# Sums of weight quarters in the first MLP matrix: accumulating transfers in a chain in place of VectorE's subtractions

## The chip, the cores and the metric

One core of a Trainium2 chip runs the whole program. The metric is the device time of one execution in microseconds (us); lower is better. The engines of the core are TensorE (PE; its weight loads are PEld), VectorE (DVE), ScalarE (ACT), GpSimd (POOL) and SyncE (SP). Each works through its own instructions in order and waits on semaphores for the others. SP and POOL also issue transfers between device memory and the on-chip memory, each into a queue of its own.

## What is computed

One layer of a decoder trunk on 512 tokens of width 2048: token mixing by a convolution and an attention branch, then a squared-ReLU MLP, with RMSNorm ahead of each and at the end. The change lies in the MLP's first product, `h @ w_ff1`, a matrix of 512 x 2048 times one of 2048 x 8192.

```python
def reference(x, g_mix, w_in, b_f, b_gate, conv_w, w_conv_out, w_attn_out,
              w_mix_out, g_mlp, w_ff1, w_ff2, g_final):
    ...
        h = rmsnorm(x, g_mlp[l])
        u = jnp.square(jax.nn.relu(jnp.einsum('bsd,df->bsf', h, w_ff1[l])))
        x = x + jnp.einsum('bsf,fd->bsd', u, w_ff2[l])
    return rmsnorm(x, g_final)
```

All inputs and the output are float32.

## The kernel before, in words

Every large product is done in 2 x 2 quarters with seven quarter products in place of eight (the scheme of Strassen and Winograd). The seven are named after the factor on the side of the activations: A11, A12, S1, S2, S3, S4, A22. A11, A12 and A22 are quarters of the activations, S1 to S4 sums and differences of them, made once and kept on chip (`Blocks.sums`, L796). The weights' quarters and their sums and differences are made anew for each block of columns.

Such a block is a `Group` (L173). For `w_ff1` there are 16 groups, g = 0 to 15, of 512 columns each. A group loads four weight quarters of 128 x 2048 floats (1 MB) by `load` (L182, SP's queue) into tiles x00, x10, x01 and x11, which take turns in four slots: `free` lists the free ones, `done` gives one back. A tile in a slot is loaded again only once everything that reads the old one has ended.

For each quarter product `run` (L194) splits its weight operand into two parts whose sum is the operand (`split`, L99): ScalarE copies it to `th` in the shorter format fp32r (L100), and VectorE takes the difference `tl` (L101). `th` and `tl` have two buffers each. Then TensorE does 48 matmuls of 128 x 128 by 256 columns (`mm_cols`, L144 to L148): 32 with `th`, 16 with `tl`. In the groups from 1 on one spare matmul stands ahead of S2 (L631).

The weight operands that are no plain quarters are made in place by VectorE with `sub` (L104), four a group, each 128 x 2048: in `tail` (L252) for groups 1 to 15, in `tail2` (L283) for group 0. `head` (L227) does A11 and A12. The order of the products is A11, A12, S4, S2, S3, S1, A22 in groups 1 to 15 and A11, A12, S1, S3, S2, S4, A22 in group 0.

The products accumulate in four PSUM banks a, b, c, d. `snap` (L205) copies a bank to a tile `o`, `plus` (L107) adds another bank to it, and `put` hands a finished quarter of the result to `put_u` (L872). That applies ReLU (L904), squares (L876), makes the sums that the second MLP matrix needs in a tile `r`, splits it into `rh` (L892) and the rest in `r` (L893), and stores both to device memory through POOL's queue (L895, L896; 896 KB each, two pairs a group). There is one tile `r` and one `rh`. `load_sums` (L938) loads them again, as `us`, through POOL's queue for the second matrix.

The instructions are given out in program order with priorities by a scheduler, so that an engine's order is fixed when the program is built.

## Time and profile before

| what | value |
|---|---|
| median of 2 runs | 2461.64 us (2461.31 to 2461.97) |
| the profiled execution, its own time | 2459.11 us |
| its span, first to last instruction | 2457.4 us |
| granted TensorE clock over the span | 0.998 |
| HBM read, written | 368.16 MB, 92.27 MB |
| the stage of the change (groups 0 to 15) | about 1230 to 1835 us |

The span is the time of the profiled execution from the first instruction to the last; 1.7 us of its own time lie around it. Busy times of engines overlap. Where one engine is busy without a gap, the others' idle time costs nothing, and a shorter instruction of theirs gains nothing unless that engine waits for it. A row of a view that groups instructions gives line, engine, operation, output and inputs, shapes, the number, then busy time in us and the mean duration of one in ns, then the idle time just before them.

### The profile page before, as it was taken

To read this page: it belongs to the slowest core of one execution; us is meant where nothing else is said; L and a number is where in the kernel's file an instruction comes from. 1 tells how busy PE (TensorE), PEld (TensorE's weight loads), DVE (VectorE), ACT (ScalarE), POOL (GpSimd) and SP (SyncE) were. 2 spreads that over 40 slices of the span, in tenths; PEclk is the share of its full clock that TensorE was granted. 3 is DMA by queue.
4 is the path that set the end of the run, shared out by engine and by line. 5 is a ranking of instruction groups with operands and counts; after the bars stand their busy time and mean duration, and the time that the engine had idled before them with its cause. 6 is when DMAs were issued, how large, how long until landed. Compare 5 with 4: busy or idle time off the path is not lost.

```text
span 2457.4 us, 39283 instructions
## 1 busy us (share of the span) xinstructions
PE 2431.6 (99%) x16928; PEld 2247.3 (91%) x16928; DVE 1921.1 (78%) x1592; ACT 1149.1 (47%) x1147; POOL 180.0 (7%) x280
## 2 busy tenths in 40 slices
PE   8999999999999999999999999999999999999998
PEld 8999999999999988888899999999998888888886
DVE  7887777788777744425688898988988888889898
ACT  6443443334444532225556666666665333333334
POOL 0100000001000000000000000000011001100000
PEclk9999999999999999999999999999999999999999
DMA  7564544456534554335645646556488576655662
GB/s 249 182 191 143 165 128 138 155 168 210 163 118 149 176 180 142 128 137 190 204 144 202 237 178 228 198 201 235 172 298 299 169 253 223 239 187 184 246 224 102
DMA packets 272036, 463.00 MB, mean 188 GB/s; under 512 B 10269, under 2 KB 172181, under 8 KB 271733
## 3 DMA queue, kind: packets, MB, share of 16 engines
q1 hardware_dynamic: 235136, 303.13, 38.3%
q0 software_dynamic: 35856, 156.25, 16.9%
q8 instruction: 133, 2.18, 0.4%
q10 hardware_dynamic: 868, 1.10, 0.1%
q14 instruction: 43, 0.34, 0.0%
HBM read 368.16 MB, written 92.27 MB: 187 GB/s over the span
## 4 chain that ended last, share of the span: by engine, by line
PE 95%; DVE 3%; issue 1%; ACT 1%; DMA 1%; POOL 0%; SPq 0%; DVEq 0%; POOLq 0%; ACTq 0%
PE a L148 6%; PE a L144 6%; PE a L146 6%; PE a L162 5%; PE a L164 5%; PE a L161 5%; PE d L148 5%; PE d L144 5%; PE d L146 5%; PE c L146 4%; PE c L144 4%; PE c L148 3%; PE d L162 3%; PE d L164 3%; PE d L161 3%; PE b L144 2%
## 5 line engine op out<-in xcount | busy, mean ns | idle before, releaser
L100 ACT ACTIVATE th<-x 128x2048 fp32r<-128x2048 f32 (+1 forms) x252 | 483.2, 1918 | 506.3 <-DVE x L104 156.5
L101 DVE TENSOR_TENSOR tl<-x,th 128x2048 fp32r<-128x2048 f32 (+1 forms) x252 | 575.6, 2290 | 172.1 <-ACT th L100 157.9
L104 DVE TENSOR_TENSOR x<-x,x 128x2048 f32<-128x2048 f32 (+1 forms) x144 | 329.7, 2289 | 8.3 <-DMA x<-in_w_in_dram 6.2
L100 ACT ACTIVATE th<-y 128x2048 fp32r<-128x2048 f32 x81 | 155.6, 1922 | 227.7 <-PE a L162 138.7
L101 DVE TENSOR_TENSOR tl<-raw,th 128x2048 fp32r<-128x2048 f32 x40 | 91.7, 2293 | 150.7 <-ACT th L100 150.1
L161 PE MATMUL a<-th,us 128*128 128x512 f32 x512 | 199.2, 389 | 0.0
L162 PE MATMUL a<-th,us 128*128 128x512 f32 x512 | 199.2, 389 | 0.0
L101 DVE TENSOR_TENSOR tl<-y,th 128x2048 fp32r<-128x2048 f32 x81 | 185.1, 2288 | 16.8 <-ACT th L100 16.6
L144 PE MATMUL a<-ST,th 128*128 128x256 f32 x752 | 173.4, 277 | 0.8 <-ACT th L100 0.8
L146 PE MATMUL a<-ST,th 128*128 128x256 f32 x752 | 172.9, 276 | 0.0
L100 ACT ACTIVATE th<-raw 128x2048 fp32r<-128x2048 f32 x40 | 76.7, 1918 | 176.3 <-PE pt L345 71.5
L144 PEld LDWEIGHTS a<-ST,th 128*128 128x128 f32 x752 | 141.2, 188 | 1.1 <-ACT th L100 1.0
L146 PEld LDWEIGHTS a<-ST,th 128*128 128x128 f32 x752 | 141.2, 188 | 0.0
L164 PE MATMUL a<-tl,us 128*128 128x512 f32 x512 | 136.7, 389 | 0.0
L144 PE MATMUL c<-S,th 128*128 128x256 f32 x576 | 134.6, 278 | 0.0
L146 PE MATMUL c<-S,th 128*128 128x256 f32 x576 | 134.4, 278 | 0.0
L100 ACT ACTIVATE th<-t 128x2048 fp32r<-128x2048 f32 x31 | 59.5, 1919 | 125.3 <-DVE t L104 73.0
L144 PE MATMUL d<-ST,th 128*128 128x256 f32 x512 | 117.7, 276 | 0.0
L146 PE MATMUL d<-ST,th 128*128 128x256 f32 x512 | 117.6, 276 | 0.0
L162 PEld LDWEIGHTS a<-th,us 128*128 128x128 f32 x512 | 96.1, 188 | 20.0
L164 PEld LDWEIGHTS a<-tl,us 128*128 128x128 f32 x512 | 96.0, 188 | 20.0
L161 PEld LDWEIGHTS a<-th,us 128*128 128x128 f32 x512 | 96.1, 188 | 20.0
(298 smaller groups left out, 6384.0 us busy)
## 6 DMA issues: line engine op xcount, KB each, us to landing
x<-in_w_in_dram SPq DMA_DIRECT2D x86, 1024.0 KB, 5.7
x<-in_w_ff_dram SPq DMA_DIRECT2D x64, 1024.0 KB, 7.2
y<-in_w_ff_dram SPq DMA_DIRECT2D x64, 1024.0 KB, 7.7
us<-s_d POOLq DMA_DIRECT2D x48, 1024.0 KB, 9.0
s_d<-rh POOLq DMA_DIRECT2D x32, 896.0 KB, 5.6
s_d<-r POOLq DMA_DIRECT2D x32, 896.0 KB, 5.8
raw<-in_w_mix_out_dram SPq DMA_DIRECT2D x24, 1024.0 KB, 5.1
g_d<-o POOLq DMA_DIRECT2D x32, 256.0 KB, 2.7
```

Source lines behind the costliest of these rows:

```text
L100: nc.scalar.activation(out=hi, in_=src, func=AF.Copy)
L101: nc.vector.tensor_tensor(out=lo, in0=src, in1=hi.bitcast(F32), op=ALU.subtract)
L104: nc.vector.tensor_tensor(out=out, in0=a, in1=b, op=ALU.subtract)
L144: nc.tensor.matmul(o, hi[:, q, js], Sh, start=first and q == 0 and j == 0, stop=False, skip_group_check=True)
L146: nc.tensor.matmul(o, hi[:, q, js], Sl, start=False, stop=False, skip_group_check=True)
L148: nc.tensor.matmul(o, lo[:, q, js], Sh, start=False, stop=q == nq - 1, skip_group_check=True)
L161: nc.tensor.matmul(o, Sh, hi[:, q, :], start=begin and q == 0, stop=False, skip_group_check=True)
L162: nc.tensor.matmul(o, Sl, hi[:, q, :], start=False, stop=False, skip_group_check=True)
L164: nc.tensor.matmul(o, Sh, lo[:, q, :], start=False, stop=q == nq - 1, skip_group_check=True)
```

## The change

The weight sums of `w_ff1` are no longer made on VectorE. A new method `chained` does a whole group:

- x00 becomes a chain. It holds the plain quarter for A11. When its split has been read, a transfer from device memory adds quarter (0, 1) onto it, which gives the weight operand of S1; after that one's split a second transfer adds (1, 1), for S2; then a third adds (1, 0), for A22. A separate transfer adds (1, 1) onto x01, for S3. So each group has four loads as before and four accumulating transfers (`onto`) of 1 MB, issued on POOL's queue.
- All weight operands are now plain sums. The signs that they had go to the activations (in `Blocks.sums` one addition becomes a subtraction and one the reverse) and to the results (`minus`, and a negative scale in a snapshot).
- The order of the products is A11, A12, S1, S3, S2, S4, A22 in all 16 groups, so that each second product reads the chain.
- In groups 1 to 15 all four quarters are loaded ahead; in group 0 (`ahead=False`) two of them. The load of the first `us` in the last group moves from behind `head` to behind the `put` of the first result quarter, which is the same place between A12 and the third product.

```diff
+        def minus(self, s, ps, scale=1.0):
+
+            p = ps[0][:, :2 * self.w].rearrange("p (b c) -> p b c", b=2)
+            if scale == 1.0:
+                sub(s, s, p)
+            else:
+                nc.vector.scalar_tensor_tensor(out=s, in0=p, scalar=-scale, in1=s, op0=ALU.mult, op1=ALU.add)
+
+        def onto(self, t, i, j):
+
+            c = self.cs[j]
+            src = self.view[:, c:c + self.w].rearrange("(q two p) c -> two p q c", two=2, p=P)
+            nc.gpsimd.dma_start(out=t, in_=src[i], accum_op=ALU.add)
...
+        def chained(self, between=lambda: None, behind=lambda: None, ahead=True):
+            X = self.X = {}
+            for ij in ((0, 0), (1, 0), (0, 1), (1, 1))[:4 if ahead else 2]:
+                X[ij] = self.load(*ij)
+            if ahead:
+                self.onto(X[0, 1], 1, 1)
+            chain = X[0, 0]
+            a = self.acc("a")
+            self.run(a, "A11", chain, True)
+            self.onto(chain, 0, 1)
+            s1 = self.snap(a)
+            between()
+            b = self.acc("b")
+            self.run(b, "A12", X[1, 0], True)
+            self.done(1, 0)
+            self.plus(s1, b)
+            self.put(0, 0, s1)
+            behind()
+            if not ahead:
+                X[0, 1], X[1, 1] = self.load(0, 1), self.load(1, 1)
+                self.onto(X[0, 1], 1, 1)
+            c = self.acc("c")
+            self.run(c, "S1", chain, True)
+            self.onto(chain, 1, 1)
+            d = self.acc("d")
+            self.run(d, "S3", X[0, 1], True)
+            self.done(0, 1)
+            d1 = self.snap(d, -self.scale)
+            self.plus(d1, c, self.scale)
+            self.run(a, "S2", chain, False)
+            self.onto(chain, 1, 0)
+            s2 = self.snap(a)
+            while later:
+                later.pop(0)()
+            self.minus(d1, a, self.scale)
+            self.put(1, 1, d1)
+            self.run(c, "S4", X[1, 1], False)
+            self.done(1, 1)
+            s4 = self.snap(c, self.scale)
+            self.minus(s4, a, self.scale)
+            self.put(0, 1, s4)
+            self.run(d, "A22", chain, False)
+            self.done(0, 0)
+            self.plus(s2, d)
+            self.put(1, 0, s2)
...
             self.put("A22", c, a22)
-            add(a22, a21, a22)
+            sub(a22, a21, a22)
...
-            sub(a12, a12, a11)
+            add(a12, a12, a11)
...
-    g0.head(True, rest)
-    Q2.sums(3)
-    g0.tail2()
+    g0.chained(rest, lambda: Q2.sums(3), ahead=False)
...
-        group.head(True, order=((0, 0), (0, 1), (1, 0)))
-        if g == DFF // S - 1:
-            us0 = {}
-            load_sums(0, (0,), us0)
-        group.tail()
+        us0 = {}
+        group.chained(behind=(lambda: load_sums(0, (0,), us0)) if g == DFF // S - 1 else lambda: None)
```

Where this puts the instructions, at three places of one pair of groups, 7 and 8. A row gives the line (the changed kernel's lines stand some 60 later than those above, L236 is `onto`, L958 and L959 are the stores of `rh` and `r`), the operation, output and inputs with their buffer numbers, the output's shape, and what the instruction waits for.

POOL before, from the first store in group 7 on:

```order
L895 DMA s_d3_79<-rh_14628 128x1792 [waits DMASW0_49,Activation_49]
L896 DMA s_d3_79<-r_14620 128x1792 [waits DMASW1_49,DVE_49]
L895 DMA s_d3_79<-rh_14926 128x1792 [waits DMASW2_49,Activation_49]
L896 DMA s_d3_79<-r_14918 128x1792 [waits DMASW3_49,DVE_49]
L895 DMA s_d3_79<-rh_15054 128x1792 [waits DMASW4_49,Activation_49]
```

POOL now, from the first link of group 7 (x00_14694 is its chain, x00_15121 and x01_15125 belong to group 8) on:

```order
L236 DMA x00_14694<-in_w_ff1_dram 128x8x256 [waits DMAHW5_49,DMAHW2_49,DVE_49]
L958 DMA s_d3_79<-rh_14634 128x1792 [waits DMASW6_49,Activation_49]
L959 DMA s_d3_79<-r_14626 128x1792 [waits DMASW7_49,DVE_49]
L236 DMA x00_14694<-in_w_ff1_dram 128x8x256 [waits DMASW5_49]
L958 DMA s_d3_79<-rh_14988 128x1792 [waits DMASW1_49,Activation_49]
L959 DMA s_d3_79<-r_14980 128x1792 [waits DMASW2_49,DVE_49]
L236 DMA x00_14694<-in_w_ff1_dram 128x8x256 [waits DMASW3_49,DMASW0_49,DVE_49]
L236 DMA x01_15125<-in_w_ff1_dram 128x8x256 [waits DMAHW0_49,DMAHW3_49,DMASW4_49,DVE_49]
L236 DMA x00_15121<-in_w_ff1_dram 128x8x256 [waits DMAHW6_49,DMAHW1_49,DVE_49]
L958 DMA s_d3_79<-rh_15061 128x1792 [waits DMASW6_49,Activation_49]
L959 DMA s_d3_79<-r_15053 128x1792 [waits DMASW7_49,DVE_49]
L236 DMA x00_15121<-in_w_ff1_dram 128x8x256 [waits DMASW5_49,DVE_49]
```

Where only stores stood, two a pair, there are now a group's four accumulating transfers among them in one queue. In group 7 the second link stands behind both stores of the pair before it, and group 8's first two transfers stand behind the third link of group 7.

VectorE before, in group 7 from the split of S4's operand on (x11_14804 and x10_14692 are weight quarters, x00_14688 is S1's operand):

```order
L101 TENSOR_TENSOR tl_14808<-x11_14804,th_14807 128x2048 [waits PE_49,Activation_49]
L893 TENSOR_TENSOR r_14620<-r_14620,rh_14628 128x1792 [waits Activation_49]
L104 TENSOR_TENSOR x11_14804<-x11_14804,x00_14688 128x2048 [waits DVE_49]
L107 TENSOR_TENSOR o_14747<-b_14749,o_14747 128x512 [waits PE_49]
L104 TENSOR_TENSOR x10_14692<-x10_14692,x11_14804 128x2048 [waits DVE_49]
L101 TENSOR_TENSOR tl_14863<-x11_14804,th_14862 128x2048 [waits Activation_49]
L101 TENSOR_TENSOR tl_14935<-x01_14690,th_14934 128x2048 [waits PE_49,Activation_49]
L107 TENSOR_TENSOR r_14918<-o_14490,r_14918 128x256 [waits DMASW1_49,Activation_49]
L104 TENSOR_TENSOR r_14918<-r_14918,o_14490 128x256
L104 TENSOR_TENSOR r_14918<-r_14918 128x256 [waits DVE_49] x2
L101 TENSOR_TENSOR tl_14989<-x00_14688,th_14988 128x2048 [waits PE_49,Activation_49]
L893 TENSOR_TENSOR r_14918<-r_14918,rh_14926 128x1792 [waits Activation_49]
```

VectorE now, in group 7 from the split of S1's operand on:

```order
L101 TENSOR_TENSOR tl_14816<-x00_14694,th_14815 128x2048 [waits DMASW5_49,PE_49,Activation_49]
L956 TENSOR_TENSOR r_14626<-r_14626,rh_14634 128x1792 [waits Activation_49]
L107 TENSOR_TENSOR o_14757<-b_14759,o_14757 128x512 [waits PE_49,Activation_49]
L101 TENSOR_TENSOR tl_14870<-x01_14698,th_14869 128x2048 [waits DMASW4_49,Activation_49]
L104 TENSOR_TENSOR r_14980<-r_14980,o_14551 128x256 [waits DMASW7_49,DVE_49,Activation_49]
L107 TENSOR_TENSOR r_14980<-o_14551,r_14980 128x256 [waits Activation_49]
L104 TENSOR_TENSOR r_14980<-r_14980 128x256 [waits DVE_49] x2
L956 TENSOR_TENSOR r_14980<-r_14980,rh_14988 128x1792 [waits Activation_49]
L101 TENSOR_TENSOR tl_14925<-x00_14694,th_14924 128x2048 [waits DMASW0_49,PE_49,Activation_49]
L101 TENSOR_TENSOR tl_14998<-x11_14700,th_14997 128x2048 [waits DMAHW0_49,PE_49,Activation_49]
L107 TENSOR_TENSOR o_14921<-c_14814,o_14921 128x512 [waits Activation_49]
L104 TENSOR_TENSOR o_14921<-o_14921,a_14703 128x512 [waits DVE_49,Activation_49]
```

The two subtractions of weight tiles among these splits are gone. What stands behind `tl` of S1 (x00_14694) is the remainder of `r` for the store that POOL has ahead of the next link. A new `r` can be begun only once the last one's store has landed, and it stands ahead of `tl` of S2.

ScalarE before, at the end of group 8, from the operand of S1 to the square of the next result:

```order
L100 ACTIVATE th_15414<-x00_15114 128x2048 [waits DVE_49,PE_49]
L892 ACTIVATE rh_15352<-r_15344 128x1792 [waits DMASW4_49,DVE_49,Activation_49]
L205 ACTIVATE o_15342<-a_15120 128x512 [waits PE_49]
L100 ACTIVATE th_15485<-x10_15118 128x2048 [waits PE_49]
L205 ACTIVATE o_15412<-d_15359 128x512 [waits PE_49]
L100 ACTIVATE th_15547<-x00_15540 128x2048 [waits DMAHW5_49,DVE_49,PE_49]
L205 ACTIVATE o_15466<-a_15120 128x512 [waits PE_49]
L904 ACTIVATE o_15412<-o_15412,common_11671 128x512 [waits DVE_49]
L876 ACTIVATE r_15472<-o_15412 128x256 [waits DMASW7_49,Activation_49]
L876 ACTIVATE o_15412<-o_15412 128x256
```

ScalarE now, at the end of group 8, from the operand of S2 to A11 of group 9 (x00_15548):

```order
L100 ACTIVATE th_15351<-x00_15121 128x2048 [waits DMASW0_49,PE_49]
L955 ACTIVATE rh_15415<-r_15407 128x1792 [waits DMASW6_49,DVE_49]
L100 ACTIVATE th_15424<-x11_15127 128x2048 [waits DMAHW4_49,PE_49]
L205 ACTIVATE o_15348<-d_15295 128x512 [waits PE_49]
L100 ACTIVATE th_15493<-x00_15121 128x2048 [waits DMASW2_49,DVE_49,PE_49]
L205 ACTIVATE o_15405<-a_15130 128x512 [waits PE_49]
L967 ACTIVATE o_15348<-o_15348,common_11671 128x512 [waits DVE_49]
L939 ACTIVATE r_15480<-o_15348 128x256 [waits DMASW3_49,Activation_49]
L939 ACTIVATE o_15348<-o_15348 128x256
L100 ACTIVATE th_15558<-x00_15548 128x2048 [waits DMAHW5_49,PE_49]
```

Before, the operand of the next group's A11 came two rows behind A22's (x10_15118), with a copy of a bank between. Now a copy, a ReLU that waits for VectorE and two squares stand between `th` of A22 (x00_15121, the third time) and `th` of the next A11.

## Prediction

> **What bounds the kernel now.** I read the page from its top, first the busy shares and the chain that ended last:
>
> ```profile
> span 2457.4 us, 39283 instructions
> ...
> PE 2431.6 (99%) x16928; PEld 2247.3 (91%) x16928; DVE 1921.1 (78%) x1592; ACT 1149.1 (47%) x1147; POOL 180.0 (7%) x280
> ...
> PE 95%; DVE 3%; issue 1%; ACT 1%; DMA 1%; POOL 0%; SPq 0%; DVEq 0%; POOLq 0%; ACTq 0%
> ```
>
> TensorE is the bound, and VectorE stands on the chain for 3%. The change lies in one stage, so the next view is the chain in order of time over that stage. Columns: start, duration, what. The rows below are the first matmul of product S2 in two groups, eight groups apart, and the low-part matmuls of two products in a row:
>
> ```profile
> 1434.17 0.14 PE a L144
> ...
> 1590.60 1.81 PE a L148 x16
> 1596.04 1.81 PE d L148 x16
> ...
> 1739.72 0.14 PE a L144
> ```
>
> A group takes (1739.72 - 1434.17) / 8 = 38.19 us, a product 1596.04 - 1590.60 = 5.44 us, of which 1.81 us are the last third, which alone needs tl. Seven products and the one spare matmul make 38.2 us, so nothing is idle between them. The timeline of TensorE shows only two waits near the stage, both in its first group:
>
> ```profile
> 1241.73 0.36 PE L137 MATMUL d<-ST,th 128*128 128x192 f32 x1 [0.83 <-ACT th L100]
> 1248.39 0.39 PE L144 MATMUL a<-ST,th 128*128 128x256 f32 x1 [0.82 <-ACT th L100]
> ```
>
> Does a busy VectorE slow the matmuls? Busy times in two stretches of 20 us that follow each other, and over the eight groups:
>
> ```profile
> core 0: us, PE busy (x) PEld busy (x) DVE busy (x) ACT busy (x) POOL busy (x), PEclk, DMA share, GB/s
> 1660.00:1680.00 20.00, 20.00 (x179) 20.00 (x178) 15.34 (x13) 14.20 (x13) 1.06 (x2) 1.00 0.78 267
> 1680.00:1700.00 20.00, 20.00 (x179) 20.00 (x178) 20.00 (x16) 11.43 (x13) 1.06 (x2) 1.00 0.41 158
> ...
> 1434.06:1739.61 305.55, 305.55 (x2699) 305.55 (x2698) 268.30 (x201) 191.59 (x193) 17.02 (x32) 1.00 0.59 207
> ```
>
> TensorE issues 179 matmuls at a granted clock of 1.00 whether VectorE works 15.34 or 20.00 us of the 20. Its pace does not depend on what the change takes away. The last row gives the transfers' share of the 16 DMA engines, 0.59.
>
> **The change, part by part.** The durations in this stage, from the groups by shape, columns: busy us, mean ns of one, idle time before:
>
> ```profile
> L101 DVE TENSOR_TENSOR tl<-x,th 128x2048 fp32r<-128x2048 f32 x90 | 205.0, 2291 | 56.9 <-ACT th L100 56.9
> L100 ACT ACTIVATE th<-x 128x2048 fp32r<-128x2048 f32 x90 | 172.6, 1918 | 139.3 <-DVE x L104 60.3 <-PE a L146 60.2 <-PE d L146 18.8
> L104 DVE TENSOR_TENSOR x<-x,x 128x2048 f32<-128x2048 f32 x52 | 119.0, 2288 | 0.0
> L893 DVE TENSOR_TENSOR r<-r,rh 128x1792 f32<-128x1792 f32 x28 | 56.6, 2022 | 0.0
> L892 ACT ACTIVATE rh<-r 128x1792 fp32r<-128x1792 f32 x28 | 47.5, 1698 | 10.2 <-ACT o L205 10.2
> L904 ACT ACTIVATE o<-o,common 128x512 f32<-128x512 f32 x54 | 37.1, 712 | 32.1 <-DVE o L107 32.1
> L104 DVE TENSOR_TENSOR r<-r 128x256 f32<-128x256 f32 x56 | 23.7, 424 | 0.5
> L895 POOL DMA_DIRECT2D s_d<-rh x28 | 14.9, 533 | 434.7 <-ACT rh L892 434.7
> L876 ACT ACTIVATE r<-o 128x256 f32<-128x256 f32 x28 | 11.5, 411 | 0.6 <-DMA s_d<-r 0.2
> L107 DVE TENSOR_TENSOR o<-c,o 128x512 f32<-128x512 f32 x14 | 9.6, 685 | 0.0
> ...
> L881 ACT ACTIVATE r<-c 128x512 f32<-128x512 f32 x14 | 8.6, 614 | 1.8 <-DMA s_d<-r 1.8
> ```
>
> *Removed:* four subtractions of weight quarters a group, 4 x 2.29 = 9.2 us of VectorE. *Added there:* from the second group on, one more operation on results, 0.69 us. VectorE is left with 8.5 us less in 38.2. TensorE does not wait for it, so this is worth 0, or at best the two waits of 0.83 and 0.82 us. The signs (add and subtract exchanged in the sums of activations, the scale of a snapshot) keep the number and the shapes of operations and cost 0, the scheduler's moves among them too; what covers them is TensorE's unbroken row. TensorE's instructions and SP's loads stay the same in number.
>
> *Added:* 64 accumulating transfers on POOL's queue, four a group, 1024 KB each. POOL itself has time: four issues at 0.53 us, as the store's, are 2.1 us a group beside the 2.1 it spends now. Three of the four form the chain: b, then S1, S2, A22 are the same tile, and each link must wait until the split of the tile before it has been read. That is the new wait, and it counts what lies in order on ACT, VectorE and POOL behind it:
>
> 1. From S1's landing to the next accumulating transfer. th 1.92, tl 2.29: 4.2 us. In groups 1, 3, 5 and so on POOL's queue has the stores of rh and r ahead, and VectorE makes that r (2.02) right after tl: 4.2 + 2.0 + 0.5 issue = 6.8 us. In the even groups 4.2.
> 2. From S2's landing to the next: 4.2 us in both.
> 3. From A22's landing to the first link of the next group. ACT is in order: th(A22) 1.92, then 0.71 + 0.41 + 0.41 of result work, th of the next A11 1.92, then its tl 2.29: 7.7 us in the odd groups. In the even ones VectorE's subtraction of a (0.69) stands behind tl(A22), and ACT's work waits for it: 4.2 + 0.7 + 1.5 + 1.9 + 2.3 = 10.6 us.
>
> Together 6.8 + 4.2 + 7.7 = 18.7 us in odd and 4.2 + 4.2 + 10.6 = 19.0 us in even groups, 18.9 on average. With L for one accumulating transfer from issue to landing, a group cannot be shorter than 3 L + 18.9. It fits under 38.2 us only up to L = 6.4 us. Beyond that TensorE waits, before S1, S2 and A22, and each us of L costs 3 us a group.
>
> *L is not in the trace.* The nearest rows: landings of plain transfers. First the loads of this stage (x, 1024 KB, 1440 to 1600 us), its stores of r, 896 KB on POOL's queue, and the same load in the projection stage, 300 to 1000 us, where less else moves; then the page's row for 256 KB and the queue's share from 1300 to 1800 us:
>
> ```profile
> DMA to landing us min/median/max: 6.0/7.8/10.9
> ...
> DMA to landing us min/median/max: 3.9/8.3/9.6
> ...
> DMA to landing us min/median/max: 5.2/5.7/10.8
> ...
> g_d<-o POOLq DMA_DIRECT2D x32, 256.0 KB, 2.7
> ...
> q1 hardware_dynamic: 54900, 55.35, 34.4%
> ```
>
> Lower end: an accumulating transfer costs no more than a plain one and finds the queues empty, L = 6.0, the shortest load of the stage: 36.9 us, hidden. A gain beyond that is excluded, since TensorE has nothing to give. At the plain median, 7.8, it is 42.3 us, 4.1 more. Upper end: the old sum must be read as well as the quarter, so the part that grows with size doubles. From 256 KB (2.7) to 1024 KB (5.7) it is 3.0 us, 4.0 for the whole; 7.8 + 4.0 = 11.8, 54.3 us, 16.1 more. I take L = 10, about the middle of 7.8 and 11.8, for a second row speaks against the low half: the engines' share. A load costs 0.344 x 500 / 55.35 = 3.1 us of all 16 engines a MB. Four more of 1.05 MB a group are 13.0 us, 0.34 on top of 0.59, if they cost what a plain one does; at 0.93 no transfer lands as quickly as at 0.59. At twice that the share would be 1.27, and the transfers alone would need 48.5 us a group. At L = 10 the chain gives 30 + 18.9 = 48.9 us, 10.7 more, close to that floor.
>
> The page "Collectives: The Full Stack" of the Trainium skill, section "The bandwidth ceiling: the fold count and why AG ≠ RS ≠ AR", says that an add inside the transfer costs nothing by itself, but needs two source reads on one ring, which halves the rate. By it L would be the 11.8 above; no run here shows it yet.
>
> *A second wait at S2.* In odd groups ACT has th(S2) behind the next r, which is begun only when the last r's store, issued 6.2 us after S1's landing, has landed: 6.2 + 8.3 (the store's median above), then 0.61 and 0.41 to fill r, three small VectorE operations of about 0.4 each, and rh 1.70, 18.4 us. S2's data come 6.8 + 10 = 16.8 us after S1's. That is 1.6 us too late, and none with a store of 3.9: between 0 and 8 x 1.6 = 13 us in all, hidden behind the link otherwise.
>
> *Moved:* in the last group two 1 MB loads of u's sums now stand ahead of a link in POOL's queue. They wait for TensorE's last use of the tile's old content and move 2 MB at 3.1 us: up to 6 us, once. In group 0 only two quarters are loaded ahead, and its chain can cost between 0 and the 10.7 of the others. These two and the wait at S2 I leave out of the sum and in the range.
>
> *The sum:* 15 groups x 10.7 = 160 us. The profiled execution took 2459.1 us, 1.7 more than its span; the median of the runs is 2461.6. 2459.1 + 160 is 2619; 2620 stands as well for the median.
>
> **Rivals.**
> *It fits* (the other side, no change). One mechanism: L at or under 6.4 us. For it: 38.2 us of room, tl of the first A11 is made early when nothing stalls, and the stage's loads reach 6.0. Against it: their median of 7.8 without the added traffic. Time: 2457 to 2462 us. It decides at L = 6.4; up to L = 7.5 the loss (3 x 1.1 x 15 = 49 us) stays within 2%.
> *Both reads in full.* L of 11 to 13 as in the upper end: at 11.8 15 x 16.1 = 242 us, 2701. For it: the share of 1.27. Against it: the second read is of on-chip memory and may run beside the first.
> *Row by row.* If the engine reads, adds and writes each 1 KB row before it takes the next, L goes beyond 13, for example to 16: 66.9 us a group, 2890. Nothing in the trace speaks for or against it.
> *VectorE's relief shows*, faster. The two rows with 179 matmuls exclude it: 2457 at best.
>
> **How the numbers follow.** It fits or nearly (L up to 7.5, 2457 to 2510 us): 0.21. Forecast (L of 7.5 to 11, 2510 to 2665): 0.47. Both reads in full (2665 to 2760): 0.22. Row by row: 0.09. Faster by over 2%: 0.01. The predicted time is the forecast's, 2620, its own range 2510 to 2665. The full range reaches down through the case that fits, 2457, and up into the doubled one, to 2715; it leaves out about 0.15. A measurement of this kernel tells 2%, 49 us, from no change. Faster 0.01, same 0.21, slower 0.78.
>
> **What would show it.** Right: TensorE idle ahead of S1, S2 and A22, ended by th, and th waiting for a transfer; 64 accumulating transfers of 9 to 11 us to landing; 48 to 49 us from one group's S2 to the next; VectorE at 25 us a group in place of 33.5. Odd groups would wait most at S2, behind the store of r. Wrong: a median landing under 7 us and groups of 38.2 us (it fits); a landing near 10 us with groups still near 38, which would mean that my count of 18.9 us is too long; or a lower granted clock.

## The result, and the profile after

The changed kernel takes 2771.23 us (median of 2 runs, 2768.96 to 2773.5) against 2461.64 us: 1.126 times as long, 95% interval 1.121 to 1.131. The prediction had 2620 us and a range up to 2715. The direction and the place were as forecast, the size was not: 310 us in place of 160.

The page of the changed kernel, first its span, busy times and clock by slice:

```profile
span 2771.8 us, 39415 instructions
...
PE 2523.5 (91%) x16928; PEld 2325.7 (84%) x16928; DVE 1797.6 (65%) x1543; ACT 1151.1 (42%) x1147; POOL 283.0 (10%) x344
...
PE   8999999999999999987877877777786899999998
...
PEclk9999999999999999999888889899898999999999
```

VectorE lost 123.5 us (1921.1 to 1797.6) and the span grew by 314.4. TensorE's row breaks in the second half, where the first MLP matrix stands, and its granted clock falls in the same slices. Next, TensorE's waits in the whole run: what waited, for what, us in total, times, longest.

```profile
PE c L144 <- ACT th L100: 84.1, 16, 10.8
PE spare L694 <- ACT th L100: 78.4, 15, 12.8
PE d L144 <- ACT th L100: 43.3, 16, 3.8
```

These are the starts of S1 (`c`), of S2 (the spare matmul stands ahead of it) and of A22 (`d`), once a group each. The page's groups and DMA issues say what th waited for; in an issue's row the last number is the median time from issue to landing:

```profile
L100 ACT ACTIVATE th<-x 128x2048 fp32r<-128x2048 f32 (+1 forms) x252 | 481.1, 1913 | 708.2 <-DMA x<-in_w_ff_dram 371.1
...
L236 POOL DMA_DIRECT2D x<-in_w_ff_dram x64 | 101.2, 1581 | 448.7 <-DVE tl L101 249.5
...
x<-in_w_ff_dram SPq DMA_DIRECT2D x64, 1024.0 KB, 10.6
x<-in_w_ff_dram POOLq DMA_DIRECT2D x64, 1024.0 KB, 11.5
```

The two rows with POOL are the 64 accumulating transfers: 1.58 us of POOL each, and 11.5 us to landing. ScalarE's split waited 371.1 us for a transfer, and POOL waited 249.5 us for VectorE's part of a split: the ring that the prediction drew, in which a transfer waits for a split, the next split for that transfer, and so on from one group into the next.

How long is a group? The spare matmul stands once in each of the groups 1 to 15, so its first and last start are 14 groups apart. Before:

```profile
L631 PE MATMUL spare<-ST,th x15: 248/248/248, 1281.2 to 1815.9; 128*128 128x192 f32 x15
```

and after:

```profile
L694 PE MATMUL spare<-ST,th x15: 355/526/529, 1318.9 to 2115.2; 128*128 128x192 f32 x15
```

(1815.9 - 1281.2) / 14 = 38.19 us before, (2115.2 - 1318.9) / 14 = 56.88 us now. The loop of 14 groups is 261.6 us longer, what comes ahead of its first S2 37.7 us (1281.2 to 1318.9), and the rest of the kernel behind it 15.1 us: 314.4 together. All later "groups" in this text are this difference divided by 14.

A link is one accumulating transfer onto the chain. POOL's timeline over one pair of groups, an even and an odd one, shows the links (start, us, and in brackets the idle time before and what ended it; the separate transfers for S3, at 1503.37 and 1559.98, are left out):

```profile
1454.26 1.55 POOL L236 DMA_DIRECT2D x<-in_w_ff_dram  x1 [4.30 <-DVE tl L101]
...
1472.49 1.58 POOL L236 DMA_DIRECT2D x<-in_w_ff_dram  x1 [9.72 <-DVE tl L101]
...
1487.37 1.55 POOL L236 DMA_DIRECT2D x<-in_w_ff_dram  x1 [0.18 <-issue]
...
1509.42 1.56 POOL L236 DMA_DIRECT2D x<-in_w_ff_dram  x1 [4.49 <-DVE tl L101]
1525.19 0.59 POOL L958 DMA_DIRECT2D s_d<-rh  x1 [14.21 <-ACT rh L955]
1527.86 0.57 POOL L959 DMA_DIRECT2D s_d<-r  x1 [2.08 <-DVE r L956]
1528.42 1.62 POOL L236 DMA_DIRECT2D x<-in_w_ff_dram  x1
...
1546.67 1.58 POOL L236 DMA_DIRECT2D x<-in_w_ff_dram  x1 [6.79 <-DVE tl L101]
...
1566.27 1.54 POOL L236 DMA_DIRECT2D x<-in_w_ff_dram  x1 [4.71 <-DVE tl L101]
```

and ScalarE's the splits that took up their landings, in the same order (the split of S2 in the second group, at 1541.82, is one row with the next):

```profile
1467.96 1.91 ACT L100 ACTIVATE th<-x 128x2048 fp32r<-128x2048 f32 x1 [7.66 <-DMA x<-in_w_ff_dram]
...
1482.83 1.91 ACT L100 ACTIVATE th<-x 128x2048 fp32r<-128x2048 f32 x1 [7.63 <-DMA x<-in_w_ff_dram]
...
1498.49 1.91 ACT L100 ACTIVATE th<-x 128x2048 fp32r<-128x2048 f32 x1 [9.87 <-DMA x<-in_w_ff_dram]
...
1521.39 1.91 ACT L100 ACTIVATE th<-x 128x2048 fp32r<-128x2048 f32 x1 [7.66 <-DMA x<-in_w_ff_dram]
...
1541.82 3.71 ACT L100 ACTIVATE th<-x 128x2048 fp32r<-128x2048 f32 x2 [4.83 <-DMA x<-in_w_ff_dram]
...
1558.41 1.91 ACT L100 ACTIVATE th<-x 128x2048 fp32r<-128x2048 f32 x1 [6.35 <-DMA x<-in_w_ff_dram]
```

From each issue to the split: 13.7, 10.3, 11.1 us in the first group, 12.0, 13.4, 11.7 in the second, 12.0 on average. What remains of the 112.0 us of the pair (1454.26 to 1566.27) is 39.7, or 19.9 us a group in which no link is under way: splits, and stores ahead in the queue. A ring of 3 x 12.0 + 19.9 us sets this pair's groups of 56.0. The same reading of all 42 links between the first and the last spare matmul gives 12.3 us from issue to split and 19.9 us a group between them: 3 x 12.3 + 19.9 is the mean group of 56.9.

### The profile page after: what moved, and what is told of

Its sections match the earlier page's. It is cut to its first block, busy times and chain, and to the rows that moved or that the text cites. A ratio compares the mean times of both kernels' runs of the same rounds, so it can differ in the third digit from the quotient of the medians.

```text
span 2771.8 us, 39415 instructions
## 1 busy us (share of the span) xinstructions
PE 2523.5 (91%) x16928; PEld 2325.7 (84%) x16928; DVE 1797.6 (65%) x1543; ACT 1151.1 (42%) x1147; POOL 283.0 (10%) x344
## 5 line engine op out<-in xcount | busy, mean ns | idle before, releaser
L100 ACT ACTIVATE th<-x 128x2048 fp32r<-128x2048 f32 (+1 forms) x252 | 481.1, 1913 | 708.2 <-DMA x<-in_w_ff_dram 371.1
L144 PE MATMUL c<-ST,th 128*128 128x256 f32 x512 | 152.6, 328 | 91.5 <-ACT th L100 84.1
L144 PEld LDWEIGHTS c<-ST,th 128*128 128x128 f32 x512 | 120.1, 235 | 95.8 <-ACT th L100 87.3
L104 DVE TENSOR_TENSOR x<-x,x 128x2048 f32<-128x2048 f32 (+1 forms) x80 | 183.2, 2289 | 7.9 <-DMA x<-in_w_in_dram 6.4
L144 PE MATMUL d<-ST,th 128*128 128x256 f32 x512 | 135.8, 303 | 43.3 <-ACT th L100 43.3
L146 PE MATMUL c<-ST,th 128*128 128x256 f32 x512 | 148.2, 320 | 0.0
L236 POOL DMA_DIRECT2D x<-in_w_ff_dram x64 | 101.2, 1581 | 448.7 <-DVE tl L101 249.5
L144 PEld LDWEIGHTS d<-ST,th 128*128 128x128 f32 x512 | 108.0, 211 | 46.5 <-ACT th L100 46.5
L144 PE MATMUL a<-ST,th 128*128 128x256 f32 x512 | 136.4, 304 | 3.8 <-ACT th L100 3.8
L146 PE MATMUL a<-ST,th 128*128 128x256 f32 x512 | 134.6, 300 | 0.0
L146 PE MATMUL d<-ST,th 128*128 128x256 f32 x512 | 133.3, 298 | 0.0
L146 PEld LDWEIGHTS c<-ST,th 128*128 128x128 f32 x512 | 119.9, 234 | 0.0
## 6 DMA issues: line engine op xcount, KB each, us to landing
x<-in_w_ff_dram POOLq DMA_DIRECT2D x64, 1024.0 KB, 11.5
```

The source lines that it names most:

```text
L100: nc.scalar.activation(out=hi, in_=src, func=AF.Copy)
L104: nc.vector.tensor_tensor(out=out, in0=a, in1=b, op=ALU.subtract)
L144: nc.tensor.matmul(o, hi[:, q, js], Sh, start=first and q == 0 and j == 0, stop=False, skip_group_check=True)
L146: nc.tensor.matmul(o, hi[:, q, js], Sl, start=False, stop=False, skip_group_check=True)
L236: nc.gpsimd.dma_start(out=t, in_=src[i], accum_op=ALU.add)
```

## The experiments

Theory: the chain is a ring from one group to the next, 3 L + T long (L is the time of an accumulating transfer from issue to landing, T the time of the splits and the queue between), and it alone sets the group. Rivals: the transfers cost by their load on the DMA engines, whoever waits; or TensorE's lower clock after each gap costs.

**All sums back on VectorE, the rest of the change kept** (order of the products, signs on the activations):

```diff
-            self.onto(chain, 0, 1)
...
+            add(chain, chain, X[0, 1])
             c = self.acc("c")
             self.run(c, "S1", chain, True)
```

and likewise for S3, S2 and A22.

> The new order of products and the new signs, but all four sums of a group made by VectorE in place, no accumulating transfer. If the transfers are the whole loss: 2455 to 2465 us, TensorE without a gap, 38.2 us a group. If the order or the signs cost something: the part of the 310 us that is theirs stays.

2465.37 us (10 runs), 1.0017 times before (1.0007 to 1.0027), group 38.19 us. In its profile the 14 groups are as long as before and the first S2 of the loop (the one in group 1) starts 7.4 us later (1288.6). Order and signs cost 4 us by the runs, ahead of the loop; everything else comes with the transfers.

**Plain copies in place of accumulating ones.** Same 64 transfers, same waits; each overwrites its tile, so the sums are left out.

```diff
-            nc.gpsimd.dma_start(out=t, in_=src[i], accum_op=ALU.add)
+            nc.gpsimd.dma_start(out=t, in_=src[i])
```

> The 64 transfers of the change as plain copies from POOL's queue: same bytes from device memory, same waits and queue places, nothing added (the weight sums are left out, so the output is not the reference's). Theory A (an accumulating transfer also reads the old sum and takes the 16 engines twice as long): landing falls from 11.5 us to 8 or 9, a group from 56.9 us to 3 x 8.5 + 20.1 = 45.6, the whole to about 2600 us. Theory B (POOL's queue, its 1.56 us issues and the 1 KB rows are what is slow, the add costs nothing): landing stays at 11 to 12 us and the time at 2771 us.

2578.92 us, 1.048 times before (1.046 to 1.050). Landings of the weight transfers of POOL's queue in the stage:

```profile
DMA to landing us min/median/max: 6.3/7.9/9.8
```

and the spare matmul:

```profile
L694 PE MATMUL spare<-ST,th x15: 248/427/529, 1301.4 to 1928.9; 128*128 128x192 f32 x15
```

The group is 44.8 us. With the median of 7.9 and the 19.9 us between links the ring gives 43.6. In the changed kernel the same view has a median of 11.5; the means over the loop, landing by landing, are 8.0 and 12.0. So the ring would cost 118 us even with plain transfers, and the add in the transfer the other 192 (2771.2 - 2578.9).

**Transfers by themselves**: first many tiles, some of them side by side, then, since those phases ran into each other, one tile, so that each transfer starts when the last has landed.

> Only transfers of one weight quarter (1024 KB, 1 KB rows) into tiles, none of the reference's computation: 8 plain loads from SP one after another, 8 plain from POOL, 8 accumulating from POOL, each waiting for the last; then 8 plain and 8 accumulating onto four tiles in turn, then 12 accumulating beside 12 loads from SP. Theory A: plain 5 to 6 us to landing, accumulating 8.5 to 10 alone; in flight together an accumulating one takes about 6 us of the engines, a plain one 3. Theory B: both alike, 6 to 8 us alone. Row by row: accumulating over 13 us alone.

Of the first only its end can be read: eight accumulating transfers with no load beside them, a median landing of 9.5 us.

> Transfers alone, one after the other on one tile, so that each starts when the last has landed; none of the reference's computation. Nine loads by SP, eight plain by POOL, eight accumulating by POOL, 1 MB each; then eight plain and eight accumulating of 512 KB. Theory: accumulating 9.5 us for 1 MB as in the transfers alone before, plain 6 to 7, the difference about 3 us (the second read of 1 MB by the engines' time a MB); 512 KB accumulating 6 to 6.5, plain 4.5 to 5. If the price were fixed and not by bytes, both sizes would differ by the same 3 us.

The second kernel's timeline of POOL, first and last row of each kind (8 plain of 1 MB, 8 accumulating, 8 plain of 512 KB, 8 accumulating; the idle time before a row is the rest of the transfer ahead):

```profile
53.76 1.06 POOL L61 DMA_DIRECT2D t<-in_w_ff_dram  x1 [53.31 <-DMA t<-in_w_ff_dram]
...
108.36 1.58 POOL L61 DMA_DIRECT2D t<-in_w_ff_dram  x1 [5.76 <-DMA t<-in_w_ff_dram]
...
187.70 0.79 POOL L61 DMA_DIRECT2D t<-in_w_ff_dram  x1 [8.41 <-DMA t<-in_w_ff_dram]
...
222.96 1.30 POOL L61 DMA_DIRECT2D t<-in_w_ff_dram  x1 [3.60 <-DMA t<-in_w_ff_dram]
...
266.94 1.27 POOL L61 DMA_DIRECT2D t<-in_w_ff_dram  x1 [5.23 <-DMA t<-in_w_ff_dram]
```

1 MB plain: (108.36 - 53.76) / 8 = 6.8 us; accumulating (187.70 - 108.36) / 8 = 9.9; 512 KB plain 4.4, accumulating (266.94 - 222.96) / 7 = 6.3. The add costs 3.1 us for 1 MB and 1.9 for half of it, so most of its price goes with the bytes. What is left at no bytes, on a line through the two sizes, is 2.0 us plain and 2.6 accumulating; the slope is 1.5 times as steep. So the 3 us that were expected held, and a price fixed for each transfer did not. Each of the two programs ran once.

**Fill TensorE's gaps.** 36, 18 and 36 free matmuls ahead of S1, S3 and S2, into a bank that nobody reads:

```diff
+            self.fill(36)
             self.run(c, "S1", chain, True)
```

> The changed kernel with 36, 18 and 36 matmuls that wait for nothing put ahead of S1, S3 and S2 in each group (about 10 us of TensorE a group, less than its idle time there), so that the gaps are shorter and the granted clock falls less. The chain bounds: group stays at 56 to 57 us, the whole at 2760 to 2785 us, clock nearer to 1.0 in the stage. Theory C (the lowered clock after each gap lengthens the loop): up to the 92 us by which TensorE's busy time grew come back, 2680 to 2740 us.

2786.14 us, 1.132 times before (1.130 to 1.135), group 57.8, just above what was expected. TensorE worked 133 us more (2656.8) and its mean clock went from 0.96 to 0.981, yet nothing was won and only 15 us lost. Its waits at S1 fell from 84.1 us to 9.8, and those at A22, where nothing was filled in, rose from 43.3 to 65.7: the ring still sets the pace. So nothing came back of what a cost of the clock would have given, up to 92 us, though the gap ahead of A22 was not filled.

**S3's sum back on VectorE**: 48 accumulating transfers, the chain kept.

```diff
-                self.onto(X[0, 1], 1, 1)
...
+            add(X[0, 1], X[0, 1], X[1, 1])
             d = self.acc("d")
             self.run(d, "S3", X[0, 1], True)
```

> The changed kernel with S3's weight sum made by VectorE (2.29 us a group) and the three links of the chain left as they are: 48 accumulating transfers instead of 64. If the three links in a row and the engines' share set the time: the first link no longer queues behind S3's transfer, landing falls from 12 us to 10.5 to 11, a group from 56.9 to 52 or 53 us, the whole to about 2700 us. If the number of accumulating transfers alone counted, a quarter of the loss would go: 2694 us as well; if S3's transfer is off the loop, nothing: 2771 us.

2730.44 us, 1.109 (1.107 to 1.112), group 54.7, less gain than expected: the median landing is 10.9 in place of 11.5, 1.8 us a group over three links, and the group lost 2.2. A quarter of the traffic gone gives back 13% of the loss (41 of 310), since it was not part of the ring and only stood in its way.

**Stores on SP's queue**, so that they stand ahead of no link (the store of `rh` likewise):

```diff
-            nc.gpsimd.dma_start(out=s_d[g // 2][:, 1, q], in_=r)
+            nc.sync.dma_start(out=s_d[g // 2][:, 1, q], in_=r)
```

> The changed kernel with the stores of rh and r issued from SP's queue instead of POOL's. In odd groups the second link then needs not wait for r: 7.1 us from S1's landing to its issue become 4.6, and its landing 13.3 becomes about 12; an odd group gains some 3.5 us, all groups 1.8 on average, 2740 to 2750 us. Against that, SP's loads now stand behind the stores' waits: if that delays them, no gain or a loss of some us a group.

2763.17 us, 1.123 (1.120 to 1.125), group 56.3: 8 us, less than expected. The median landing is no shorter (12.1).

**First group on VectorE, and u's first load behind the last chain.**

> The changed kernel, but group 0's sums made by VectorE and the first load of us put behind the last group's chain. Groups 1 to 15 unchanged. Expected: the stage's start loses its 38 us (group 0 and up to S2 of group 1 back to about 52 to 60 us from 90), the last group's second link lands in 12 us instead of 17.8 and gives back about 5 us: 2725 to 2735 us. If group 0's loss only moves into group 1: 2755 to 2771 us.

2740.05 us, 1.113 (1.111 to 1.115). The first spare matmul starts at 1299.5 in place of 1318.9, and the part behind the last is 647.7 us in place of 656.6. So the first group's chain costs about 19 us and u's load and its wake about 9; 5 us came from the loop.

**One accumulating transfer a group that is not in a ring.** First S3's alone, with the chain on VectorE and S1 as x00 + x01 - x11, since x01 holds the sum by then:

> The opposite of the kernel before last: S3's sum by an accumulating transfer ahead, the chain's sums by VectorE (five operations of 2.29 us a group, since S1's is made as x00 + x01 - x11). 16 accumulating transfers, none on a loop. If the loop is what costs, this is hidden: 38.2 us a group, 2455 to 2475 us. If accumulating transfers cost TensorE or the other transfers by themselves: a quarter of the loss, 2530 us or more.

2605.26 us, 1.058 (1.056 to 1.060): far from what was expected. The waits of TensorE show why:

```profile
PE b L148 <- DVE tl L101: 89.4, 15, 7.5
```

S1's sum now needs x01 after its transfer, and that sum stands ahead of A12's split in VectorE's order; x01's load waits for a slot that the group before frees. The transfer had been put into a ring again, through VectorE. The experiment doesn't answer its question. The next takes A22's sum alone, two products after S2's split (the edit against the version with all sums on VectorE):

```diff
-            add(chain, chain, X[1, 0])
+            self.onto(chain, 1, 0)
```

> The new order with the sums of S1, S3 and S2 by VectorE; only A22's sum is made by an accumulating transfer (16 of 64), with two products between S2's split and A22's. No landing of one group then releases the next group's transfer. Theory 'the loop costs, not the transfer': 2463 to 2480, as with all sums on VectorE (2465.4) and at most a few us of waits where a landing takes over 12 us. Rival 'each accumulating transfer costs by itself' (its engine time or its effect on the other loads, (2771.2-2465.4)/4 = 76 us for a quarter of them): 2530 to 2550.

2613.61 us, 1.063 (1.061 to 1.065), group 47.3. That is slower than either side had forecast. The waits:

```profile
PE d L144 <- ACT th L100: 46.2, 16, 5.6
PE b L148 <- DVE tl L101: 17.6, 14, 1.8
PE c L144 <- DVE o L107: 17.5, 15, 1.2
PE spare L692 <- ACT th L100: 13.1, 14, 2.1
```

TensorE waits 2.9 us a group for A22's sum, so two products and the lead of a split are not enough for 11 us of landing. Behind it come waits that all sums on VectorE do not have, 48 us at three other products, and its matmuls take 44 us more (2480.1 busy against 2435.9). Together with the 46 us that is 138 of the 145 us by which the spans differ. What ties the waits at the other products to A22's is not traced here.

**The same traffic with nobody waiting.** Is the rest the transfer's load on the engines? All sums on VectorE, and an accumulating transfer of 1 MB beside them onto tiles in DRAM that nothing uses, one or four a group:

> All sums by VectorE in the new order (2465.4 alone), and beside them one accumulating transfer of 1 MB a group (16, as many as where A22's sum alone is made by transfer) onto tiles in DRAM whose contents nothing uses: the stage's traffic rises, nobody waits for it. Left out: nothing of the computation. Theory 'the cost of A22's sum by transfer (2613.6) is the wait for its landing and what the wait does to the engines behind it': 2465 to 2485. Rival 'an accumulating transfer slows the loads beside it enough to cost by itself': 2560 to 2620.

> The same with four such transfers a group (64), waited for by nobody. Theory 'the 16 DMA engines have a limit of their own near 46 us a group, which the halved transfers (2594.6) reached': the loads come late and the time is 2570 to 2630 though no sum is waited for. Rival 'the engines have room, and the halved transfers were held by the chain still': 2465 to 2520.

2533.16 us (1.030, 1.028 to 1.031) and 2694.15 us (1.095, 1.093 to 1.097), and neither answers: nothing held these transfers, so they ran in the first stages of the kernel and delayed those. In the stage itself the group was 38.19 us in both. Tied to their group by a 1 KB transfer of a result row onto the same tile:

> As with the transfers aside before, which turned out to run ahead of the whole stage since nothing held them; now each is tied to its group by a 1 KB transfer of a result row onto its tile ahead of it. All sums by VectorE, one accumulating transfer of 1 MB a group (16) onto tiles in DRAM that nobody reads. Theory 'the cost of A22's sum by transfer (2613.6) is the wait and what it does behind it': group 38.2 to 38.8 us, 2465 to 2480. Rival 'an accumulating transfer slows the loads and so costs by itself': group 44 to 47 us, 2560 to 2615.

2479.55 us (1.009, 1.007 to 1.010). The spare matmul:

```profile
L702 PE MATMUL spare<-ST,th x15: 248/248/253, 1284.6 to 1834.2; 128*128 128x192 f32 x15
```

and the issues between 1400 and 1800 us:

```profile
x<-in_w_ff_dram SPq DMA_DIRECT2D x41, 1024.0 KB, 7.0
...
side<-in_w_ff_dram POOLq DMA_DIRECT2D x10, 1024.0 KB, 9.5
```

39.3 us a group: an accumulating transfer whose sum nobody waits for, with its tie, costs about 1 us here, the loads beside it still land in 7.0 us, and it takes 9.5. So such traffic explains some 14 of A22's 148 us. 46 of the others are the wait itself; that the rest follows from the wait is argued from the rows above, not measured alone. (Destination DRAM, not the on-chip tile: the traffic is alike, not the same.)

> The same with four a group (64). Theory 'the 16 DMA engines are a second limit': the loads land late, the group is 44 to 49 us, 2560 to 2640, with the engines busy over 95% of the stage. Rival 'the engines have room for four, only waits cost': group 38.2 to 40 us, 2465 to 2500.

2715.08 us (1.103, 1.101 to 1.105), group 53.3, outside both forecasts. The tied 1 KB transfers land behind the accumulating one ahead of them in POOL's queue, 8.4 us, and ScalarE's ReLU waits 336.6 us for them, since they read the tile that it changes. But the loads beside them also landed later, 12.1 us in place of 7.0 (1300 to 1800 us of both). The two prices can't be told apart here, so what four such transfers a group cost without a wait stays open.

**Halves.** Each link as two transfers of 512 KB, and the splits of the chain's products in two halves, so that one half's transfer is under way while the other is split:

```diff
-            nc.gpsimd.dma_start(out=t, in_=src[i], accum_op=ALU.add)
+            for q in range(2):
+                h = slice(q * KT // 4, (q + 1) * KT // 4)
+                nc.gpsimd.dma_start(out=t[:, h], in_=src[i][:, h], accum_op=ALU.add)
```

> Each accumulating transfer is cut into two of 512 KB, and the splits of the chain's four products into two halves each, so that a half of the next sum can be under way while the other half is split. Theory 'the time from issue to landing and the hops bound the loop, the engines have room': the group falls from 56.9 us to between 49 and 53, 2650 to 2715 in all. Rival 'the engines are the limit at 12 us a transfer': the group stays at 55 to 58, 2745 to 2790.

2594.62 us, 1.055 (1.053 to 1.056), group 46.1: better than expected, 57% of the loss gone with not a byte less. The engines' busy share by slice in the stage, 1300 to 1800 us:

```profile
DMA  9999999999989999999999999999999999999899
```

That looks like a second limit at 46 us, the engines. The test: S3's sum back on VectorE in this kernel.

> The halved chain (2594.6, group 46.1 us, DMA engines full), but S3's sum by VectorE: 48 MB of accumulating transfers in place of 64. Theory 'with halves the DMA engines are the limit': their time a group falls by about a quarter of the accumulating share, 0.787 x 46.1 / 4 = 9 us less at most, so the group comes to 39 to 42 us, 2490 to 2540. Rival 'the chain is still the limit with halves': group 45 to 46.5 us, 2580 to 2600.

2596.51 us, 1.056 (1.054 to 1.057), the group again 46.1. The spare matmul:

```profile
L696 PE MATMUL spare<-ST,th x15: 252/356/529, 1295.3 to 1941.3; 128*128 128x192 f32 x15
```

and the two kernels from 1300 to 1800 us, first with all sums by transfer, then with S3's on VectorE (the last three numbers are TensorE's granted clock, the engines' share and GB/s):

```profile
1300.00:1800.00 500.00, 444.04 (x3658) 437.09 (x3659) 286.48 (x283) 267.28 (x304) 136.24 (x129) 0.96 1.07 264
1300.00:1800.00 500.00, 448.20 (x3682) 442.18 (x3682) 310.73 (x296) 267.71 (x306) 109.19 (x109) 0.96 0.95 241
```

With a quarter of the accumulating traffic gone the engines carry less, 241 GB/s in place of 264, and the time is the same: in the second kernel it isn't what they can carry that sets the time. But this doesn't show that the same chain is the limit in both. The halves landed sooner, 6.6 us in place of 8.5, and the gain went elsewhere. The profile's chain of work that ended last goes through a store's landing in the first kernel, ahead of a split of the chain:

```profile
1481.47 9.42 DMA s_d<-r
```

and in the second through a plain load, for which VectorE's new addition waits:

```profile
1449.81 7.03 DMA x<-in_w_ff_dram
...
1456.86 2.29 DVE x L107
```

Both are rings of transfers that wait for each other, and that they come out alike may be chance. Nor is a share near 1 a limit by itself: it reads 1.07 here, over 1, and in two neighbouring windows of the changed kernel 1.23 at 206 GB/s and 1.13 at 334 (last section). It counts packets under way, not what could be carried.

No version beats the kernel before. TensorE had nothing to give there, and the best of the new order is the one without transfers, 2465.4 us.

## Why the prediction was wrong, step by step

| step | predicted | measured |
|---|---|---|
| VectorE's relief | 0, 25 us a group | 0; 123.5 us less in all, as worked out (8.5 x 15 = 127) |
| order and signs | 0 | 4 us |
| where TensorE waits | S1, S2, A22 | the same, 84.1, 78.4 and 43.3 us |
| T, between the links | 18.9 us | 19.9 |
| L | 10 us | 12.0 in the pair shown, 12.3 in the loop |
| group | 48.9 us | 56.9 |
| odd groups, second wait at S2 | 0 to 13 us in all | none |
| group 0, and group 1 up to its S2 | 0 to 10.7, and two links of a group's 10.7 | 37.7 |
| behind the loop: one link, u's load | one link of a group's 10.7, and up to 6 us | 15.1 |

**L is the step that failed.** The mechanism was right: TensorE waits where the prediction said, and the ring is the one that it drew. The term L was too small. It was put at the middle of 7.8 and 11.8, and the upper end, 7.8 + 4.0 for a second read, is what came: 12.0, or 12.3 over the whole loop. The prediction had two rows that pulled apart, the plain landing and the engines' share, and averaged the ends instead of asking how the two add up. The experiments say how: 3.1 us for the add alone (9.9 against 6.8 in series), 3.9 in the stage (mean landing 12.0 against 8.0 with plain copies), and the rest is what plain transfers in this place cost over an empty queue. L counts three times a group, so 2.3 us are 7 us a group and 98 us in the loop's 14 groups.

The Trainium skill, page "Collectives: The Full Stack", section "The bandwidth ceiling: the fold count and why AG ≠ RS ≠ AR", gives two source reads on one ring and half the rate. By it L is the prediction's 11.8 us, and the stage comes near, 12.0. Alone it does not come out so: the part that goes with the bytes grew by half, from 4.8 to 7.3 us a MB, not twofold. So the near agreement in the stage is partly luck.

**T** was 1 us short, 14 us in the loop. The stores did stand ahead of the second link in odd groups, as the rows at 1525.19 to 1528.42 show. S2's split did not wait behind r's store: the row at 1541.82 follows the landing at once, and so does its like in the other seven odd groups. The prediction's price of 1.6 us had too short an L in it; with the longer one the store was done in time. In the kernel with halves, where a link is shorter, such a store did come onto the path (the row at 1481.47).

**Group 0** was the worst term after L. It was bounded by the loss of another group, 10.7 us. Of the 37.7 us ahead of the first S2 of the loop, 7 are the new order by itself (1288.6 with all sums on VectorE) and 19 are group 0's own chain, by the kernel that takes it off (1299.5). Why it costs more than another group is argued only: the first has just two quarters loaded ahead, and its chain starts behind a late load. The remaining 11 us (1299.5 against 1288.6) lie in the first links of group 1, which the prediction had in its 15 groups; this is argued from the order and not measured alone. Behind the loop u's load and its wake took 9 us where up to 6 were allowed.

**The floor of 48.5 us** from the engines' share, which spoke for L = 10, was no floor: with halves the same bytes went through in 46.1 us. It took a plain load's share of the engines, doubled, as a price of capacity; the share, which read 1.07 in that kernel, is none.

**The lower clock** was on the prediction's list of signs against it, and it came, 0.96 in place of 0.998. It followed TensorE's gaps, and filling two of the three in each group won nothing back.

**The sum with the measured terms:** 14 x (56.9 - 38.2) + 37.7 + 15.1 = 314 us on the profiled 2457.4, the measured span. Of a group's 56.9 us, 48.9 were forecast, 7 are L and 1 is T.

The rival *Both reads in full* (11.8 us a link, 54.3 us a group, 2701) had the loop nearly right and lacked the two ends. *Row by row* fell. *It fits* would have needed landings of 6.4 us; even plain ones alone take 6.8.

## What to carry to other kernels

A sum moved from an engine into a chain of dependent transfers trades that engine's time for latency: count what lies on the way round (landing, split, queue, issue) and compare it with the period, before asking whether queues and engines have room. Price a landing under the traffic that the change itself adds: where an empty-queue price and a share near one pulled apart here, the upper one came, and it is multiplied by the links. And here cutting the links into halves that overlap shortened the chain far more than taking traffic from beside it, 177 us against 41.

## What the runs showed of the hardware

After the longer of its gaps TensorE's granted clock (the column behind POOL's) fell to half. Windows of 4 us in the changed kernel; a gap of 4.33 us lies at the end of the second row and in the third:

```profile
1460.00:1464.00 4.00, 4.00 (x36) 4.00 (x35) 1.91 (x1) 0.30 (x1) 0.69 (x2) 1.00 1.23 206
1464.00:1468.00 4.00, 1.60 (x14) 1.39 (x12) 0.00 (x0) 0.04 (x1) 0.00 (x0) 1.00 1.13 334
1468.00:1472.00 4.00, 2.08 (x9) 2.08 (x10) 2.10 (x1) 4.00 (x3) 0.00 (x0) 0.64 1.00 397
1472.00:1476.00 4.00, 4.00 (x20) 4.00 (x20) 4.00 (x6) 2.34 (x5) 1.58 (x1) 0.50 0.45 90
1476.00:1480.00 4.00, 4.00 (x37) 4.00 (x36) 0.43 (x2) 0.00 (x0) 0.00 (x0) 1.00 1.18 185
```

At 0.50 TensorE issued 20 matmuls in 4 us, at 1.00 it issues 37. How long must a gap be? Two shorter ones behind it, with the windows in which they end:

```profile
1484.80 0.36 PE L694 MATMUL spare<-ST,th 128*128 128x192 f32 x1 [0.89 <-ACT th L100]
1500.45 0.58 PE L144 MATMUL d<-ST,th 128*128 128x256 f32 x1 [2.86 <-ACT th L100]
```

```profile
1484.00:1488.00 4.00, 3.20 (x28) 3.20 (x29) 3.22 (x2) 4.00 (x3) 1.19 (x2) 1.00 0.09 35
1500.00:1504.00 4.00, 3.55 (x19) 3.55 (x20) 2.89 (x2) 1.53 (x3) 0.63 (x1) 0.59 0.43 154
```

After 0.89 us the clock stayed, after 2.86 it fell, and so it was with the others looked at, in windows of 1 us: 1.23 and 2.14 us left it at 1.00, 2.88, 3.51 and 4.98 us brought it down. It stayed down for some 3.3 us (after 2.86, 2.88 and 3.51) or some 6.7 (after 4.33 and 4.98). The page "TensorE: Matmul & The Clock Gate" of the Trainium skill, section "Part 1: The HAM clock gate (the "warmup" mystery)", has half speed after an idle window of about 3.4 us and full speed after a busy one as long. The trace agrees on the half and on the length of one or two such windows; a gap shorter than 3.4 us was enough here. In the ring this was free as far as the filled gaps show. Where A22's sum alone was late, the waits were 2.9 us a group and the matmuls still took 44 us more in all.

An accumulating transfer costs POOL 1.58 us to issue, where the prediction put the 0.53 of a store; a plain one of the same shape took 0.88 in the series alone. It lies within L here, since L counts from the start of the issue. And transfers that nothing holds back run where the scheduler finds room: 64 unneeded ones at the start of the kernel cost 229 us there without any reader.
